# Two gated MLPs entered differently: the mixer's last products and the first plain pair in one loop, a second plain pair, no GpSimd work at the entries

## Chip, cores and metric

One core of a Trainium2 chip runs the whole program in one launch. The metric is the device time in microseconds (us); three runs of the kernel before took 2312.16, 2318.49 and 2319.06 us, so the median is 2318.49 us. TensorE (PE in the rows) multiplies matrices, VectorE (DVE), ScalarE (ACT) and GpSimd (POOL) work elementwise, and SyncE (SP) issues the DMAs.

## What is computed

The reference is an encoder of two layers on one sequence of 1024 frames with 1024 channels. Each layer is a mixer and a gated MLP, each behind an RMS norm and each added to the residual stream. The change touches only the seams between mixer and MLP:

```python
def conv_ffn(h, w_up, conv_w, conv_b, w_down):
    s = h.shape[1]
    u = h @ w_up                                  # 1024 -> 2 x 2816
    up = jnp.pad(u, ((0, 0), (CONV_WIDTH - 1, 0), (0, 0)))
    conv = conv_b
    for j in range(CONV_WIDTH):
        conv = conv + conv_w[j] * up[:, j:j + s]
    a, g = jnp.split(conv, 2, axis=-1)
    return (jax.nn.silu(a) * g) @ w_down
...
x = x + even_mixer(...)   # layer 0; ends in "... @ w_out"
x = x + conv_ffn(rms_norm(x, ffn_norm[layer]), ...)
x = x + odd_mixer(...)    # layer 1; ends in "... @ w_out"
x = x + conv_ffn(rms_norm(x, ffn_norm[layer]), ...)
```

## The kernel before

Everything is transposed: a tile has 128 channels on the partitions and 1024 frames along it, so the residual stream `x` is eight tiles, `x[0]` to `x[7]`. `T0` and `T1` are a tile's left and right 512 frames, and a product over 512 frames fills one bank of PSUM. TensorE works in the rounded 32-bit format fp32r; for accuracy each operand is split into a high part (ScalarE, a cast) and a low part (VectorE, a subtraction), and each product is three matmuls, high by high, high by low and low by high (`mm3`, L137, L139 and L141).

**End of a mixer.** The last two of eight inner tiles of the mixer's output product are applied tile by tile of `x`, in the order 0, 4, 1, 5, 2, 6, 3, 7 (`ORDER`): for each tile two halves of 2 x 3 matmuls into PSUM, then VectorE adds the bank to `x` (L745 in layer 0, L761 in layer 1). That is 8 x 12 = 96 matmuls.

**Norm and blocks.** After each tile `NormBlocks.add` stores `x` to DRAM for the later residual (L288), writes the tile times its gain as two split blocks (`blk`: high part by ScalarE at L282, low part by VectorE at L283), squares it on ScalarE (L302) and adds the square to a running sum (L303, on GpSimd for all but the last tile). Then ScalarE scales `x` itself by the gain (L304), for use in sums of blocks. `stats` (L254) sums the squares over the partitions by 16 tiny matmuls, ScalarE and VectorE turn that into 1/rms, a diagonal tile is built (L261), and `spread` (L268, L269) broadcasts it to `rstd_bc`.

**Up-projection.** There are 22 pairs of an `a` tile and a gate tile (`FT` = 22). Pair 0 is plain: all eight blocks against two weight tiles, 2 x 48 = 96 matmuls, loaded and split by `raw_a` (L781, L782). VectorE then multiplies the banks by `rstd_bc` (L909). Pairs 1 to 21 save products with a Strassen-like scheme (`Pair`, L823): seven products of 12 matmuls, 84 for a pair. It needs sums of the weights (`s12`, `s34`, L794 to L799, loaded two pairs ahead through `wraw` and `raw_g`) and sums of the blocks of `x` (L914 to L917, on GpSimd for two of four k and on VectorE for the other two), split into `T1` to `T4` (L803). Each finished pair goes through the convolution (L886 on ScalarE, L887 and L889 on VectorE), SiLU, and the product with the gate on GpSimd (L981), and is stored to DRAM. The convolution's results rotate through three buffers, `c`.

**What sets the order.** TensorE's instructions stand in program order. Those of the other engines are ordered at build time by a list scheduler; on the chip each engine runs its own list strictly in order and waits by semaphores. So an instruction that waits holds up all that stands behind it on its engine. PSUM has eight banks, two each for `lin`, `z`, `t` and `d`. The blocks and the mixer's last operands share 16 buffers, so the blocks of the last two tiles reuse those of the operands.

Of the kernel before, what the change touches and what calls it, by code (L numbers as in the profile page):

```python
# [56 lines left out]
def trunk_kernel(  # L57
# [213 lines left out]
    class NormBlocks(Norm):  # L271
# [14 lines left out]
        def add(self, m, x):  # L286
# [10 lines left out]
            if self.n == 1:  # L297
                self.acc = self.acc_tile()
                S.activation(self.acc, x, AF.Square)
            else:  # L300
                sq = self.sq_tile()
                S.activation(sq, x, AF.Square)  # L302
                (V if self.n == KT else G).tensor_tensor(self.acc, self.acc, sq, op=ALU.add)  # L303
            S.activation(x, x, AF.Copy, scale=g)  # L304
# [433 lines left out]
    for m in ORDER:  # L738
        sl = slice(m * P, (m + 1) * P)
        for i, cs in enumerate(HALVES):  # L740
            ps = bank(("lin", "z")[i])
            for n, k in enumerate(last):
                mm3([ps], (ws[n][0][:, sl], ws[n][1][:, sl]), ([mix[k][0][:, cs]], [mix[k][1][:, cs]]),
                    n == 0, n == len(last) - 1)
            V.tensor_tensor(x[m][:, cs], x[m][:, cs], ps, op=ALU.add)  # L745
        norm.add(m, x[m])
# [3 lines left out]
    def accumulate(ws, acts, tags, after=None, order=range(KT), together=1):  # L750
        order = list(order)
        n = len(ws)
        for ms in [order[:together]] + [[m] for m in order[together:]]:
            pss = {m: [bank(next(tags)), bank(next(tags))] for m in ms}
            for i, cs in enumerate(HALVES):
                for m in ms:
                    sl = slice(m * P, (m + 1) * P)
                    for k in range(n):
                        mm3([pss[m][i]], (ws[k][0][:, sl], ws[k][1][:, sl]),
                            ([acts[k][0][:, cs]], [acts[k][1][:, cs]]), k == 0, k == n - 1)  # L760
                    V.tensor_tensor(x[m][:, cs], x[m][:, cs], pss[m][i], op=ALU.add)  # L761
            if after is not None:
                for m in ms:
                    after(m)

    def ffn(layer, nm, after, onward=None):
# [72 lines left out]

        def scaled(dst, cs):  # L840
# [52 lines left out]
        pss = []  # L893
        for i in (0, FT):
            _, hi, lo = raw_a(i)
            ps = [bank(next(tags)), bank(next(tags))]
            for n, k in enumerate(ORDER):
                rt = (nm.b11[k], nm.b12[k]) if k < 4 else (nm.b21[k - 4], nm.b22[k - 4])
                sl = slice(k * P, (k + 1) * P)
                mm3(ps, (hi[:, sl], lo[:, sl]), ([t[:, T0] for t in rt], [t[:, T1] for t in rt]),  # L900
                    n == 0, n == KT - 1)
                if i and n == 3:
                    nm.stats(next(tags))
            pss.append(ps)
        nm.spread(tags)
        us = [slot(F32, "u") for _ in range(2)]
        for u, ps in zip(us, pss):
            for cs, b in zip(HALVES, ps):
                V.tensor_tensor(u[:, cs], b, rstd_bc[:, cs], op=ALU.mult)  # L909
        load_a(1)  # L910
        for k in range(4):
            E = TENG(k)
            lo_, hi_ = x[k], x[k + 4]
            E.tensor_tensor(lo_[:, T0], lo_[:, T1], lo_[:, T0], op=ALU.subtract)  # L914
            E.tensor_tensor(lo_[:, T1], hi_[:, T1], lo_[:, T1], op=ALU.subtract)
            E.tensor_tensor(hi_[:, T1], hi_[:, T1], lo_[:, T0], op=ALU.subtract)
            E.tensor_tensor(hi_[:, T0], hi_[:, T0], hi_[:, T1], op=ALU.subtract)  # L917
        sum12(1)
# [454 lines left out]
```

## Time and profile before

| | |
|---|---|
| median of three runs | 2318.49 us (2312.16 to 2319.06) |
| the profiled execution's own time | 2324.55 us |
| its span, first to last instruction | 2322.8 us |
| busy shares: PE, DVE, ACT, POOL | 96%, 72%, 44%, 18% |
| mean granted TensorE clock | 0.977 of full |
| entry of layer 0 (mixer's last products to end of pair 1) | 446.48 to 536.51 us |
| entry of layer 1 (the same) | 1598.12 to 1686.48 us |

A busy share is an average over stages. What the change touches are two stretches of some 90 us each, called the entries here, and a change there is worth what TensorE waits there, whatever the averages say. In a row of the timeline the first number is the start in us from the span's start, the second the length, then engine, source line, operation, output and inputs, and in brackets how long the engine was idle before and what ended that. A row of stretches has, for each engine, busy us and instructions, then the granted clock (PEclk), the DMA engines' share and GB/s.

### The profile page before, as it was taken

The numbers are of one execution on the slowest core, as the hardware profiler recorded it, in microseconds if no ns is written. First come the engines' busy times: TensorE is split into PE (matmuls) and PEld (weight loads), VectorE is DVE, ScalarE is ACT, GpSimd is POOL, SyncE is SP. The second block draws the span as 40 slices with busy tenths as digits, with TensorE's granted clock in tenths as the row PEclk, the third lists the DMA queues.
The fourth block names the chain that finished last, engine by engine and source line by source line (L and its number), as shares of the span: only waits on it lengthen the run. The fifth ranks groups of instructions, "written<-read, shape, count | busy, mean of one in ns | idle before, by whom it ended". The sixth has DMA issues, their size and how long they took to land.

```text
span 2322.8 us, 27350 instructions
## 1 busy us (share of the span) xinstructions
PE 2236.1 (96%) x10624; PEld 1840.3 (79%) x10624; DVE 1664.0 (72%) x2221; ACT 1031.8 (44%) x1561; POOL 421.6 (18%) x250
## 2 busy tenths in 40 slices
PE   8999889979999999999999999999799999999999
PEld 7878777758888887888887878787588888878887
DVE  5576588698999998745446555557999999986543
ACT  6666666454444444311146352527544444442210
POOL 2331350131111111512020000003211111124210
PEclk9999889979999999999999999999899999999999
DMA  3000112222222225522001111112222222254211
GB/s 140 19 29 20 38 35 99 87 82 73 82 82 82 82 82 177 183 85 91 10 28 41 34 46 36 41 43 87 68 82 82 82 82 82 82 199 163 95 51 73
DMA packets 51425, 178.52 MB, mean 77 GB/s; under 512 B 5968, under 2 KB 6608, under 8 KB 51296
## 3 DMA queue, kind: packets, MB, share of 16 engines
q1 hardware_dynamic: 51296, 176.78, 22.7%
q8 instruction: 83, 1.36, 0.2%
q14 instruction: 46, 0.38, 0.1%
HBM read 140.06 MB, written 36.70 MB: 76 GB/s over the span
## 4 chain that ended last, share of the span: by engine, by line
PE 82%; DVE 9%; issue 3%; ACT 3%; DMA 1%; POOL 0%; SPq 0%; DVEq 0%; ACTq 0%; POOLq 0%
PE lin L823 15%; PE z L823 10%; PE lin L137 5%; PE t L823 5%; PE d L823 5%; PE lin L139 5%; PE lin L141 5%; PE z L141 2%; PE t L139 2%; PE z L139 2%; PE z L137 2%; PE t L137 2%; PE t L141 2%; PE d L139 2%; PE d L137 2%
## 5 line engine op out<-in xcount | busy, mean ns | idle before, releaser
L123 ACT CAST whi<-wraw 128x1024 fp32r<-128x1024 f32 (+4 forms) x108 | 107.6, 998 | 356.5 <-PE d L139 233.3
L981 POOL TENSOR_TENSOR c<-c 128x1024 f32<-128x1024 f32 x44 | 108.3, 2461 | 757.9 <-ACT c L980 757.9
L841 DVE TENSOR_TENSOR u<-u,rstd_bc 128x512 f32<-128x512 f32 x168 | 168.2, 1002 | 2.8
L124 DVE TENSOR_TENSOR wlo<-wraw,whi 128x1024 fp32r<-128x1024 f32 (+3 forms) x94 | 137.3, 1460 | 35.2 <-ACT whi L123 34.3
L886 ACT ACTIVATE c<-u,prm 128x1024 f32<-128x1024 f32 x88 | 109.4, 1246 | 84.4 <-DVE u L841 74.3
L1010 POOL TENSOR_TENSOR act<-a,act 128x1024 fp32r<-128x1024 f32 x40 | 105.8, 2653 | 217.2 <-ACT act L1009 217.2
L610 DVE TENSOR_TENSOR_SCAN pt<-pt,z 128x128 f32<-128x128 f32 (+3 forms) x96 | 93.1, 970 | 55.7 <-ACT z L603 53.1
L137 PE MATMUL lin<-h_hi,whi 128*128 128x512 f32 x304 | 122.4, 441 | 5.9 <-ACT whi L123 5.9
L823 PE MATMUL d<-T,a 128*128 128x512 f32 x504 | 121.1, 389 | 0.0
L889 DVE SCALAR_TENSOR_TENSOR c<-u,prm,c 128x1022 f32<-128x1022 f32 x88 | 115.6, 1315 | 0.1
L887 DVE SCALAR_TENSOR_TENSOR c<-u,prm,c 128x1023 f32<-128x1023 f32 x88 | 112.4, 1279 | 2.9 <-ACT c L886 2.7
L761 DVE TENSOR_TENSOR x<-x,t 128x512 f32<-128x512 f32 x97 | 66.4, 685 | 65.5 <-PE t L141 65.4
L139 PE MATMUL lin<-h_lo,whi 128*128 128x512 f32 x304 | 111.7, 405 | 1.3 <-DVE h_lo L240 1.3
L141 PE MATMUL lin<-h_hi,wlo 128*128 128x512 f32 x304 | 111.7, 406 | 0.0
L823 PE MATMUL lin<-blk,whi 128*128 128x512 f32 x336 | 107.8, 403 | 3.2 <-DVE u L909 3.2
L823 PEld LDWEIGHTS d<-T,a 128*128 128x128 f32 x504 | 94.6, 188 | 19.6
L802 ACT CAST s12h<-s 128x1024 fp32r<-128x1024 f32 x42 | 44.2, 1054 | 146.1 <-PE lin L823 142.5
L823 PE MATMUL z<-blk,s34h 128*128 128x512 f32 x336 | 105.6, 395 | 2.8 <-DVE u L872 2.8
L761 DVE TENSOR_TENSOR x<-x,d 128x512 f32<-128x512 f32 x97 | 66.4, 685 | 58.0 <-PE d L141 58.0
L823 PE MATMUL z<-blk,s12h 128*128 128x512 f32 x336 | 105.7, 396 | 0.0
L823 PE MATMUL lin<-T,s12h 128*128 128x512 f32 x336 | 104.5, 392 | 0.0
L823 PE MATMUL t<-blk,whi 128*128 128x512 f32 x336 | 103.6, 390 | 0.0
(406 smaller groups left out, 6497.5 us busy)
## 6 DMA issues: line engine op xcount, KB each, us to landing
wraw<-in_wup SPq DMA_DIRECT2D x46, 512.0 KB, 3.6
act<-c SPq DMA_DIRECT2D x44, 512.0 KB, 2.6
wraw<-in_wdn SPq DMA_DIRECT2D x44, 512.0 KB, 3.7
raw_g<-in_wup SPq DMA_DIRECT2D x42, 512.0 KB, 3.6
a<-act SPq DMA_DIRECT2D x40, 512.0 KB, 4.3
xs<-x SPq DMA_DIRECT2D x16, 512.0 KB, 2.6
x<-xs SPq DMA_DIRECT2D x16, 512.0 KB, 5.0
x<-in_xT SPq DMA_DIRECT2D x8, 512.0 KB, 6.6
```

The lines of the kernel that those rows point to most:

```text
L123: S.copy(hi[:, cs], raw[:, cs])
L124: (eng or V).tensor_tensor(lo[:, cs], raw[:, cs], hi[:, cs].bitcast(F32), op=ALU.subtract)
L137: PE.matmul(out[i], wh, ah[i], start=first, stop=False)
L139: PE.matmul(out[i], wh, al[i], start=False, stop=False)
L141: PE.matmul(out[i], wl, ah[i], start=False, stop=last)
L761: V.tensor_tensor(x[m][:, cs], x[m][:, cs], pss[m][i], op=ALU.add)
L823: PE.matmul(ps, w, m, start=first and k == 0 and n == 0, stop=k == 3 and n == 2, skip_group_check=True)
L841: V.tensor_tensor(dst, dst, rstd_bc[:, cs], op=ALU.mult)
L886: S.activation(c, u, AF.Identity, scale=pcol(b + 2), bias=pcol(b + 3))
L887: V.scalar_tensor_tensor(c[:, 1:], u[:, :T - 1], pcol(b + 1), c[:, 1:], op0=ALU.mult, op1=ALU.add)
L889: V.scalar_tensor_tensor(c[:, 2:], u[:, :T - 2], pcol(b), c[:, 2:], op0=ALU.mult, op1=ALU.add)
L981: G.tensor_tensor(ca, ca, cg, op=ALU.mult)
```

## The change

- `NormBlocks.add` gives all its running sums to VectorE, and scales only tiles 0 to 3 of `x` by the gain. For tiles 4 to 7 the gain is folded into the sums of blocks (`rsums`), which now all run on VectorE: one plain and three scalar-tensor-tensor instructions for each k. GpSimd has nothing left at the entries: 14 instructions leave it for each.
- The weights of pair 0 are no longer loaded through `wraw` late; they go straight into `s12` and `s34` and are split into `s12h`, `s12l`, `s34h`, `s34l` ahead of the loop.
- One loop over the tiles: the mixer's products for two tiles ahead, then for each further tile its mixer products (12 matmuls), and behind them the plain products of pair 0 that read the blocks two tiles back (12 matmuls). Two more plain tiles follow the loop.
- Pair 1 is plain too. Its `a` tile runs between `stats` and `spread`, its gate tile behind `spread`. It costs 96 matmuls where the scheme took 84. Strassen pairs start at pair 2.
- In layer 1 the mixer's operands take buffers of the block pool and its second weight one of the general weight buffers, since the attention's pool is now closed before the loop.

```diff
-                (V if self.n == KT else G).tensor_tensor(self.acc, self.acc, sq, op=ALU.add)
-            S.activation(x, x, AF.Copy, scale=g)
+                V.tensor_tensor(self.acc, self.acc, sq, op=ALU.add)
+            if m < KT // 2:
+                S.activation(x, x, AF.Copy, scale=g)
...
+        def rsums(k):
+            lo_, hi_, g = x[k], x[k + 4], pcol(nm.col + k + 4)
+            V.tensor_tensor(lo_[:, T0], lo_[:, T1], lo_[:, T0], op=ALU.subtract)
+            V.scalar_tensor_tensor(lo_[:, T1], hi_[:, T1], g, lo_[:, T1], op0=ALU.mult, op1=ALU.subtract)
+            V.scalar_tensor_tensor(hi_[:, T1], hi_[:, T1], g, lo_[:, T0], op0=ALU.mult, op1=ALU.subtract)
+            V.scalar_tensor_tensor(hi_[:, T0], hi_[:, T0], g, hi_[:, T1], op0=ALU.mult, op1=ALU.subtract)
...
+        first = []
+        for i, hl, raw, tag in ((0, (s12h, s12l), s12, "lin"), (FT, (s34h, s34l), s34, "z")):
+            nc.sync.dma_start(raw, wup[layer, i])
+            split(*hl, raw)
+            first.append((hl, [bank(tag), bank(tag)]))
...
+        def first_tile(n):
+            for w, ps in first:
+                plain_tile(w, ps, n)
...
+        add_tiles(ow, mixt, otags, ORDER[:2])
+        for n, m in enumerate(ORDER):
+            if n >= 2:
+                add_tiles(ow, mixt, otags, [m])
+            nm.add(m, x[m])
+            if n >= 2:
+                first_tile(n - 2)
+        for k in range(4):
+            rsums(k)
+            for n in ("T4", "T2", "T3"):
+                rblock(n, k)
+        first_tile(KT - 2)
+        first_tile(KT - 1)
+        nm.stats("t")
+        ps = plain(1, "td")
+        nm.spread(iter("dt"))
...
+        for b in [b for _, b in first] + [ps]:
+            evacuate(b)
+        ps = plain(FT + 1, ("lin", "z"))
         for k in range(4):
-            E = TENG(k)
...
+            rblock("T1", k)
+        load_a(2)
...
-            g = gated(hd, oraw, ss)
+            g = gated(hd, oraw, ss, hpool, "h", 16)
...
-            accumulate(out_weights(hd), mixt, itertools.cycle("td"), lambda m: nnorm.add(m, x[m]), ORDER, 2)
+            ow = [load_split(woo[2 * hd]), load_split(woo[2 * hd + 1])]
```

**How the lists move.** Nothing moves outside the two entries. On TensorE in layer 0 the kernel before goes from the mixer's products of the last tile straight to pair 0, whose first weight is `whi`:

```order
L137 MATMUL z<-mh,whi 128x512
L139 MATMUL z<-ml,whi 128x512
L141 MATMUL z<-mh,wlo 128x512
L137 MATMUL lin<-blk,whi 128x512
L137 MATMUL z<-blk,whi 128x512
L139 MATMUL lin<-blk,whi 128x512
```

Now each tile's mixer products (`d<-mh`) have a tile of pair 0 behind them, out of `s12h` and `s34h`:

```order
L137 MATMUL d<-mh,whi 128x512
L139 MATMUL d<-ml,whi 128x512
L141 MATMUL d<-mh,wlo 128x512
L137 MATMUL lin<-blk,s12h 128x512 x2
L139 MATMUL lin<-blk,s12h 128x512 x2
L141 MATMUL lin<-blk,s12l 128x512 x2
L137 MATMUL z<-blk,s34h 128x512 x2
L139 MATMUL z<-blk,s34h 128x512 x2
L141 MATMUL z<-blk,s34l 128x512 x2
```

So 12 matmuls that wait only for blocks of two tiles back lie between any two additions to `x`.

On VectorE the same place in layer 0, now; `x_3543` and `x_4115` are tiles 0 and 4, `x_3635` is tile 1, and `blk_4498` and `blk_4501` are the left and the right block of tile 0:

```order
L751 TENSOR_TENSOR x_3543<-x_3543,t_4464 128x512
L751 TENSOR_TENSOR x_4115<-x_4115,t_4466 128x512
L283 SCALAR_TENSOR_TENSOR blk_4498<-x_3543,prm_77,blk_4498 128x512
L797 TENSOR_TENSOR s12l_4450<-s12_4447,s12h_4449 128x1024
L751 TENSOR_TENSOR x_3543<-x_3543,d_4465 128x512
L797 TENSOR_TENSOR s34l_4452<-s34_4448,s34h_4451 128x1024
L751 TENSOR_TENSOR x_4115<-x_4115,d_4467 128x512
L788 TENSOR_TENSOR s12_4447<-raw_g_4446 128x512
L797 TENSOR_TENSOR a22_4453<-raw_g_4446,a22_4453 128x512
L751 TENSOR_TENSOR x_3635<-x_3635,t_4518 128x512
L283 SCALAR_TENSOR_TENSOR blk_4501<-x_3543,prm_77,blk_4501 128x512
```

The two splits of pair 0's weights and two steps for pair 2 came in ahead of the right block of tile 0, which the first plain tile reads.

On ScalarE in layer 1, now, at the same place; `s12h_12812` is the high part of pair 0's first weight, whose load must wait for the attention's buffers, and `blk_12861` the first block:

```order
L1270 CAST mh_12734<-r32_12436 128x512
L1270 CAST mh_12736<-r32_12686 128x512
L796 CAST s12h_12812<-s12_12810 128x1024
L282 ACTIVATE blk_12861<-x_7553,prm_77 128x512
L796 CAST s34h_12814<-s34_12811 128x1024
```

The cast that waits for the load stands ahead of the first block.

More of the change, by code (lines that the diff above doesn't have):

```diff
@@ new lines, in first_tile, with plain @@
+        def first_tile(n):
+            for w, ps in first:
+                plain_tile(w, ps, n)
+        def plain(i, tags):
+            w, ps = raw_a(i)[1:], [bank(t) for t in tags]
+            for n in range(KT):
+                plain_tile(w, ps, n)
+            return ps
+        otags = itertools.cycle("td")
+        add_tiles(ow, mixt, otags, ORDER[:2])
[5 more added lines that the diff above has]
+                first_tile(n - 2)
@@ L947, in ffn @@
                 ua, ug = us[0], us[1]
+            elif i == 1:
+                ua, ug = us[2], us[0]
+                for cs, b in zip(HALVES, ps):
+                    V.tensor_tensor(ug[:, cs], b, rstd_bc[:, cs], op=ALU.mult)
             else:
@@ L1040, in trunk_kernel @@
     norm.sq_tile = lambda: slot(F32, "nsq")
-    ffn(0, n0, lambda m: norm.add(x[m]), onward)
+    ffn(0, n0, lambda m: norm.add(x[m]), ws, [mix[k] for k in last], onward)
     ev = ExitStack()
```

98 lines of the change are left out of this document (33 added, 65 removed).

## The prediction

> **What bounds the kernel now.** The page's row of engines gives TensorE 96% of the span, so only stretches in which it waits can yield anything. I then cut both entries into stretches (columns: us, then busy us of PE, PEld, DVE, ACT and POOL, the granted clock, DMA share, GB/s).
>
> ```profile
> PE 2236.1 (96%) x10624; PEld 1840.3 (79%) x10624; DVE 1664.0 (72%) x2221; ACT 1031.8 (44%) x1561; POOL 421.6 (18%) x250
> ```
>
> ```profile
> 460.40:474.20 13.80, 9.94 (x30) 7.01 (x30) 13.80 (x11) 8.93 (x12) 13.80 (x8) 0.78 0.28 115
> 474.20:490.00 15.80, 7.43 (x22) 5.46 (x22) 15.77 (x15) 10.62 (x14) 10.13 (x5) 0.65 0.28 100
> 490.00:511.20 21.20, 19.17 (x94) 15.80 (x92) 19.62 (x29) 12.30 (x17) 0.00 (x0) 1.00 0.24 75
> ```
>
> From 460.4 to 474.2 VectorE is busy all 13.80 us and so is GpSimd, while TensorE gets 30 matmuls done and its clock drops to 0.78. VectorE is the bound there. The waits of TensorE, first in entry 0, then in entry 1, name what it waits for:
>
> ```profile
> PE lin L141 <- DVE wlo L782: 5.4, 1, 5.4
> PE lin L137 <- DVE x L745: 3.9, 2, 2.7
> ...
> PE lin L139 <- DVE blk L283: 5.9, 1, 5.9
> ```
>
> Why VectorE is late, its rows tell. The same split of a block takes 0.75 us at 450.50 with GpSimd idle, and 2.29 us at 460.26 with GpSimd at work; the addition to `x`, which has one input in PSUM, keeps its 0.67 us beside it.
>
> ```profile
> 450.50 0.75 DVE L283 SCALAR_TENSOR_TENSOR blk<-x,prm,blk 128x512 fp32r<-128x512 f32 x1
> ...
> 459.67 0.67 DVE L745 TENSOR_TENSOR x<-x,z 128x512 f32<-128x512 f32 x1
> 460.26 2.29 DVE L283 SCALAR_TENSOR_TENSOR blk<-x,prm,blk 128x512 fp32r<-128x512 f32 x1
> ```
>
> ```profile
> L283 DVE SCALAR_TENSOR_TENSOR blk<-x,prm,blk 128x512 fp32r<-128x512 f32 x16 | 25.3, 1593 | 1.5 <-ACT blk L282 1.5
> ```
>
> In entry 0 the 16 splits take 25.3 us where 16 x 0.74 = 11.8 would do: 13.5 us lost beside GpSimd. The Trainium skill ("SBUF — State Buffer", Who interferes with whom) says that a VectorE instruction with two SBUF inputs and a GpSimd one that reads SBUF lock each other out; these rows agree.
>
> **What the entries last, and their floor.** TensorE's rows at both ends of each entry:
>
> ```profile
> 446.48 0.39 PE L137 MATMUL z<-mh,whi 128*128 128x512 f32 x1
> ...
> 459.85 0.39 PE L141 MATMUL lin<-mh,wlo 128*128 128x512 f32 x1
> ...
> 501.72 1.84 PE L254 MATMUL lin<-ones,nacc 128*128 128x2 f32 x16
> 503.43 0.47 PE L137 MATMUL t<-blk,whi 128*128 128x512 f32 x1
> ...
> 511.19 1.12 PE L268 MATMUL z<-ndg,ones 128*128 128x512 f32 x2 [2.03 <-DVE ndg L261]
> ...
> 514.74 1.22 PE L823 MATMUL lin<-blk,whi 128*128 128x512 f32 x2 [1.08 <-DVE u L909]
> ...
> 519.74 0.63 PE L823 MATMUL z<-blk,s12h 128*128 128x512 f32 x2
> ...
> 536.51 0.62 PE L823 MATMUL lin<-blk,whi 128*128 128x512 f32 x2
> ```
>
> ```profile
> 1598.12 0.48 PE L137 MATMUL t<-mh,whi 128*128 128x512 f32 x1
> ...
> 1686.48 0.62 PE L823 MATMUL lin<-blk,whi 128*128 128x512 f32 x2
> ```
>
> Entry 0 lasts 536.51 - 446.48 = 90.0 us, entry 1 lasts 1686.48 - 1598.12 = 88.4 us. At full clock 59 matmuls start in 459.85 - 446.48 = 13.37 us, 0.2267 us each. Before, an entry holds 96 + 96 + 84 = 276 of them, 62.6 us of work, so some 27 and 26 us go to waits, slow clock and the norm. After, it holds 96 + 96 + 96 = 288, 65.3 us: the plain second pair costs 12 x 0.2267 = 2.7 us for each entry, and nothing hides that, since it is TensorE's own work.
>
> **VectorE's account.** I price its list for an entry by the steps from start to start:
>
> ```profile
> 489.66 0.74 DVE L283 SCALAR_TENSOR_TENSOR blk<-x,prm,blk 128x512 fp32r<-128x512 f32 x1
> 490.32 0.68 DVE L917 TENSOR_TENSOR x<-x 128x512 f32<-128x512 f32 x1
> 490.92 0.68 DVE L803 TENSOR_TENSOR T<-x,T 128x512 fp32r<-128x512 f32 x1
> 491.52 1.22 DVE L303 TENSOR_TENSOR nacc<-nacc,nsq 128x1024 f32<-128x1024 f32 x1
> 492.66 0.68 DVE L914 TENSOR_TENSOR x<-x 128x512 f32<-128x512 f32 x1
> ```
>
> A half tile takes 0.60 us, with a gain in it 0.66, a whole tile 1.14. What comes over from GpSimd is six sums and eight sums of blocks: 6 x 1.14 + 2 x 0.60 + 6 x 0.66 = 12.0 us, less than the 13.5 us that go. The two other plain sums of blocks per k become scalar-tensor-tensor at 0.06 us more each; ScalarE loses four scalings. Up to the first use of `rstd_bc` VectorE then has 16 additions (9.6), 16 block splits (10.6), 7 sums (8.0), 16 sums of blocks (10.3), 12 splits T2 to T4 (7.2), 6 half tiles of weight sums (3.6) and 8 whole tiles, weight splits and the diagonal among them (9.1), with the reciprocal 58.6 us, from about 1.4 us behind the entry's start: done at 60.0. In the same time TensorE has 240 matmuls and the statistics, 54.4 + 1.7 = 56.1 us. So VectorE's load stays; what the change buys is that TensorE has 48 more matmuls to do meanwhile, and that these need blocks two tiles old instead of the last ones. Both are then nearly full, and every bubble of VectorE counts almost one to one.
>
> **What TensorE still waits for.** I walk the lists with these steps.
> - First plain tile: TensorE wants the low part of tile 0's right block 36 + 3 matmuls in, at 8.8 us. VectorE has, from 2.75 us on, six half-tile steps besides two block splits and the two weight splits ahead of it: 6 x 0.60 + 2 x 0.66 + 2 x 1.14 = 7.2 us, so 10.0. Wait: 1.2 us.
> - Seventh plain tile: its blocks take over buffers of the mixer's operands and so wait for the last mixer matmul. One plain tile (2.7 us) covers; VectorE needs 5.35 us from there (an addition, a sum of blocks and a weight split stand between), TensorE wants it at 3.4. Wait: 1.9 us.
> - The turn from pair 1's first tile over `spread` to its gate tile: cast and split of pair 2's weight stand ahead of the evacuation (1.05 + 1.14), then the evacuation and a second one, with the gaps between engines 3.4 us. It was 514.74 - 511.19 = 3.55 besides a wait of 2.03 ahead of it.
> - Pair 2: the convolution of pair 1's gate reuses a `c` buffer. ScalarE has it ahead of the copy that releases TensorE's seventh product, and it waits for GpSimd's product of pair 0 and its store:
>
> ```profile
> 526.80 1.28 ACT L980 ACT_TABLE_LOAD   x1
> 528.09 1.07 ACT L980 ACTIVATE c<-c 128x1024 f32<-128x1024 f32 x1
> ```
>
> ```profile
> 529.24 2.65 POOL L981 TENSOR_TENSOR c<-c 128x1024 f32<-128x1024 f32 x1 [41.37 <-ACT c L980]
> ```
>
> ```profile
> L886 ACT ACTIVATE c<-u,prm 128x1024 f32<-128x1024 f32 x88 | 109.4, 1246 | 84.4 <-DVE u L841 74.3
> ...
> act<-c SPq DMA_DIRECT2D x44, 512.0 KB, 2.6
> ```
>
> From pair 1's last matmul on, ScalarE casts a weight (1.05), loads a table (1.28) and does SiLU (1.07); GpSimd multiplies (2.65) and the store lands (2.6); then come the convolution (1.25), a cast (1.05) and the copy (half a cast and more, 0.6): 11.5 us, wanted behind four products of 12, at 10.9. With gaps I take 0.8; the ends are nothing and, with a store of twice the time, 3.4.
>
> Pair 0's weights cost nothing in entry 0. Their loads follow this one in SyncE's queue (the second row has how long such a load takes to land):
>
> ```profile
> 437.33 0.33 SPq L778 DMA_DIRECT2D wraw<-in_wup  x1
> ```
>
> ```profile
> wraw<-in_wup SPq DMA_DIRECT2D x46, 512.0 KB, 3.6
> ```
>
> Four loads of 3.6 us, even one after the other, are there 14.4 us on, at 451.7, and the first plain tile begins at 446.5 + 8.2 = 454.7; the splits are in VectorE's account. If that cover were gone, each us of delay would show, as in layer 1.
>
> Entry 0: 65.3 + 1.7 + 1.2 + 1.9 + 3.4 + 0.8 = 74.3 us, against 90.0: 15.7 us gained. Entry 1 adds two things.
>
> ```profile
> 1597.30 1.05 ACT L781 CAST whi<-wraw 128x1024 fp32r<-128x1024 f32 x1 [4.21 <-PE z L139]
> ...
> 1601.47 0.72 ACT L282 ACTIVATE blk<-x,prm 128x512 fp32r<-128x512 f32 x1
> ...
> 1598.96 1.22 DVE L782 TENSOR_TENSOR wlo<-wraw,whi 128x1024 fp32r<-128x1024 f32 x1
> ```
>
> The mixer's second weight now takes the place of that weight in the lists, so its low part is there at 1600.1, and TensorE wants it five matmuls in, at 1599.25: 0.9 us. And pair 0's weight can be loaded only when the attention's last transposes are over, about 1598.1; landing 3.6 us later its cast ends at 1602.8, and the first block, behind it on ScalarE, comes 1.4 us later than the row at 1601.47. With three loads at once it may land later: 0 to 6 us, I take 1.4, by the median landing. Entry 1: 74.3 + 0.9 + 1.4 = 76.6 against 88.4, gain 11.8. Together 27.5 us.
>
> **The clock.** Rows of entry 0 behind a wait:
>
> ```profile
> 468.94 0.79 PE L137 MATMUL lin<-mh,whi 128*128 128x512 f32 x1 [2.70 <-DVE x L745]
> 469.53 0.63 PE L139 MATMUL lin<-ml,whi 128*128 128x512 f32 x1
> ...
> 473.80 0.63 PE L141 MATMUL z<-mh,wlo 128*128 128x512 f32 x1
> ```
>
> After idle times of 2.70 and 2.03 us matmuls start every 4.27 / 10 = 0.427 us for a while; behind the `spread` the 12 up to 519.74 took 5.0 instead of 2.7 us. One such stretch costs 2.3 us. My waits are of 0.8 to 3 us, so I count one in the two entries: 27.5 - 2.3 = 25.2. The Trainium skill ("TensorE: Matmul & The Clock Gate", What's actually happening) has the slow clock follow an idle window of about 3.4 us; by that no wait of mine brings one, and the gain would be 27.5. The rows show it after shorter ones, and I go by them.
>
> The profiled execution took 2324.55 us, so the sum against it is 2299.4. It lies 6.1 us above the median of 2318.49; from that, 25.2 us less is 2293.
>
> **Rivals.**
> A bubble of VectorE in the trace, for the second:
>
> ```profile
> 500.42 0.69 DVE L795 TENSOR_TENSOR s<-s,wraw 128x512 f32<-128x512 f32 x1 [1.55 <-DMA wraw<-in_wup]
> ```
>
> 1. The waits vanish, as the lists have slack that my walk misses. Only work, statistics and a turn of 3.0 us remain, 70.0 us for each entry: gain 20.0 + 18.4, time 2280. For it: VectorE runs back to back for long where GpSimd is idle. Against: its 58.6 us are more than TensorE's 56.1. Chance 0.12.
> 2. VectorE trails: three bubbles in each entry like that one, 6 x 1.55 = 9.3 us, and three slow stretches more, 6.9 us, leave 9.0 us of gain: 2309. For it: ScalarE's list now interleaves splits, sums and stores that wait on one another. Against: TensorE's waits would leave VectorE time to catch up. Chance 0.18.
>
> 3. The long splits were not GpSimd's doing and stay: 13.5 us in each entry, on a full VectorE, 25.2 - 27.0, about 2320. Against it stand the rows at 459.67 and 460.26, and 490 to 511.2, where all splits are short. Chance 0.04.
> 4. Slower: the loop never warms up. If each of its tiles waits some 2 us for blocks, the clock stays low, and the 168 matmuls of each loop take 0.2 us more each: 67 us. From 126 of these 336 on the gain is gone; all of them give 2318 - 25 + 67 = 2360. Against: each tile has 24 x 0.2267 = 5.4 us of TensorE's work, and what VectorE must do for it is 2 x 0.60 + 2 x 0.66 + 1.14 = 3.7 us, so waits come at single tiles. Chance 0.05.
>
> **The numbers.** The forecast, a single walk with its own errors of 8 us, has 0.61; its time is 2293. The range reaches to rivals 1 and 2, from 2280 to 2309, as bubbles and slow stretches may come in any number between. A measurement of this kernel tells about 0.3% or 7 us from no change. Faster by more: 0.61 + 0.12 + 0.18, less 0.01 for the end of rival 2 near no change, 0.90; the same 0.05; slower 0.05.
>
> **What would show it.** GpSimd without a row in both entries; all block splits near 0.74 us; entries of about 74 and 77 us; VectorE still busy nearly throughout; TensorE's waits at the first and the seventh plain tile and at pair 1's gate tile, no longer a 5 us one. Splits that stay long would refute the first step; an entry of over 85 us with short splits, the account of VectorE; a difference outside the entries, the whole frame.

## The result, and the profile after

The kernel after takes 2294.32 us (median of four runs, 2291.6 to 2299.12), the kernel before 2318.76 us in the runs beside it: a ratio of 0.99, with an interval of 0.9885 to 0.9915, so 24.4 us less, where the prediction had 25.2. Run again later (e11), the kernel after took 2294.37 us, a ratio of 0.9903 (0.9883 to 0.9923).

The row of engines on the page of the kernel after shows GpSimd's share gone down and TensorE's up by one point:

```profile
PE 2221.9 (97%) x10648; PEld 1830.4 (80%) x10648; DVE 1642.7 (72%) x2229; ACT 1018.0 (44%) x1543; POOL 364.6 (16%) x222
```

The stretches of the kernel after, entry 0, pair 2 behind it, entry 1, pair 2 behind it (us, then busy us of PE, PEld, DVE, ACT and POOL, the granted clock, DMA share, GB/s):

```profile
439.60:513.10 73.50, 70.58 (x309) 56.40 (x308) 71.48 (x99) 45.98 (x60) 0.00 (x0) 1.00 0.25 87
513.10:535.30 22.20, 19.85 (x86) 15.64 (x86) 18.52 (x18) 9.88 (x12) 5.61 (x2) 1.00 0.20 71
1573.20:1648.30 75.10, 71.12 (x311) 56.42 (x309) 74.31 (x104) 47.96 (x64) 0.00 (x0) 1.00 0.30 105
1648.30:1671.90 23.60, 21.19 (x86) 16.82 (x85) 18.60 (x18) 9.92 (x12) 5.71 (x2) 0.93 0.22 69
```

The same four of the kernel before:

```profile
445.10:536.50 91.40, 75.89 (x297) 58.60 (x296) 82.26 (x92) 53.86 (x70) 31.57 (x15) 0.87 0.23 81
536.50:555.80 19.30, 19.30 (x86) 15.81 (x85) 18.10 (x20) 9.09 (x11) 2.41 (x1) 1.00 0.26 84
1598.10:1686.50 88.40, 73.02 (x300) 56.43 (x299) 82.83 (x96) 54.29 (x73) 32.21 (x15) 0.92 0.26 90
1686.50:1705.70 19.20, 19.20 (x85) 15.76 (x84) 18.10 (x20) 8.98 (x11) 2.41 (x1) 1.00 0.29 86
```

Entry 0 begins 1.4 us earlier here than in the prediction: the first six matmuls of tile 0 write a bank that bears the same name, `lin`, as the stage ahead of them, and were counted there as part of that stage. So entry 0 lasted 91.4 us before, not 90.0. The entries lose 17.9 and 13.3 us; pair 2, untouched by the change itself, gains 2.9 and 4.4. Together 218.3 - 194.4 = 23.9 us, which is what the medians say. VectorE is busy 97% of entry 0 where it was 90%, and the granted clock is 1.00 where it was 0.87 and 0.92. The two profiled executions differ by more, 33.0 us; the other 9 us lie in parts that the change doesn't touch, and runs of one kernel differ by as much (those of the kernel before, beside e1 to e4, lie between 2310.26 and 2325.61).

The waits of TensorE in the kernel after, entry 0 and then entry 1 (total, times, longest):

```profile
PE lin L139 <- DVE blk L283: 2.0, 2, 1.2
PE lin L137 <- DVE u L940: 0.8, 1, 0.8
```

```profile
PE lin L139 <- DVE blk L283: 2.3, 2, 1.6
PE lin L137 <- DVE u L940: 0.8, 1, 0.8
PE t L141 <- DVE wlo L124: 0.7, 1, 0.7
```

The block splits of entry 0 are short now (count; ns of one: least, median, longest), where the kernel before had 737, 1514 and 2945 ns:

```profile
L283 DVE SCALAR_TENSOR_TENSOR blk<-x,prm,blk x16: 747/754/764, 443.1 to 481.9; 128x512 fp32r<-128x512 f32 x16
```

The waits of 5.4 and 5.9 us are gone, and what is left are the waits that the walk named: the first and the seventh plain tile (L139), the gate tile of pair 1 (L137) and, in layer 1, the low part of the mixer's second weight.

### The profile page after: what moved, and what is told of

Same layout as the page of the kernel before. It is cut to its first block, busy times and chain, and to the rows that moved or that the text cites. A ratio compares the mean times of both kernels' runs of the same rounds, so it can differ in the third digit from the quotient of the medians.

```text
span 2289.9 us, 27345 instructions
## 1 busy us (share of the span) xinstructions
PE 2221.9 (97%) x10648; PEld 1830.4 (80%) x10648; DVE 1642.7 (72%) x2229; ACT 1018.0 (44%) x1543; POOL 364.6 (16%) x222
## 4 chain that ended last, share of the span: by engine, by line
PE 68%; DVE 3%; issue 3%; ACT 2%; DMA 1%; POOL 0%; ACTq 0%; POOLq 0%; DVEq 0%
PE lin L817 14%; PE z L817 9%; PE d L817 5%; PE t L817 4%; PE lin L137 3%; PE lin L139 3%; PE lin L141 3%; PE z L137 3%; PE z L141 3%; PE z L139 3%; PE t L137 2%; PE d L137 2%; PE d L139 2%; PE t L139 2%; PE t L141 2%
## 5 line engine op out<-in xcount | busy, mean ns | idle before, releaser
L843 DVE TENSOR_TENSOR u<-u,rstd_bc 128x512 f32<-128x512 f32 x160 | 160.4, 1004 | 2.6
L888 ACT ACTIVATE c<-u,prm 128x1024 f32<-128x1024 f32 x88 | 109.6, 1245 | 76.8 <-DVE u L843 71.3
L137 PE MATMUL lin<-h_hi,whi 128*128 128x512 f32 x304 | 121.4, 437 | 6.3 <-ACT whi L123 6.2
L891 DVE SCALAR_TENSOR_TENSOR c<-u,prm,c 128x1022 f32<-128x1022 f32 x88 | 120.3, 1367 | 0.1
L751 DVE TENSOR_TENSOR x<-x,t 128x512 f32<-128x512 f32 x105 | 72.0, 686 | 66.9 <-PE t L141 66.8
L817 PE MATMUL d<-T,a 128*128 128x512 f32 x480 | 115.5, 389 | 0.0
L751 DVE TENSOR_TENSOR x<-x,d 128x512 f32<-128x512 f32 x105 | 72.0, 686 | 57.5 <-PE d L141 57.5
L139 PE MATMUL lin<-h_lo,whi 128*128 128x512 f32 x304 | 110.9, 403 | 1.2 <-DVE h_lo L240 1.2
L817 PE MATMUL z<-blk,s34h 128*128 128x512 f32 x320 | 100.7, 396 | 4.6 <-DVE u L874 4.6
L817 PE MATMUL lin<-T,s34h 128*128 128x512 f32 x320 | 99.9, 394 | 3.5 <-ACT tm L865 3.5
L817 PE MATMUL z<-blk,s12h 128*128 128x512 f32 x320 | 100.7, 396 | 0.0
L817 PE MATMUL lin<-blk,whi 128*128 128x512 f32 x320 | 99.8, 393 | 0.0
L817 PE MATMUL lin<-T,s12h 128*128 128x512 f32 x320 | 99.5, 392 | 0.0
```

Source lines behind the costliest of these rows:

```text
L137: PE.matmul(out[i], wh, ah[i], start=first, stop=False)
L139: PE.matmul(out[i], wh, al[i], start=False, stop=False)
L817: PE.matmul(ps, w, m, start=first and k == 0 and n == 0, stop=k == 3 and n == 2, skip_group_check=True)
L843: V.tensor_tensor(dst, dst, rstd_bc[:, cs], op=ALU.mult)
L888: S.activation(c, u, AF.Identity, scale=pcol(b + 2), bias=pcol(b + 3))
L891: V.scalar_tensor_tensor(c[:, 2:], u[:, :T - 2], pcol(b), c[:, 2:], op0=ALU.mult, op1=ALU.add)
```

## The experiments

All kernels, by rows of their traces: us of each entry, to the end of pair 1, and of pair 2 behind it; the sum of the four; the median; the ratio to the kernel before, run beside it.

| kernel | entry 0 | pair 2 | entry 1 | pair 2 | sum | median | ratio (interval) |
|---|---|---|---|---|---|---|---|
| before | 91.4 | 19.3 | 88.4 | 19.2 | 218.3 | 2318.76 | |
| after | 73.5 | 22.2 | 75.1 | 23.6 | 194.4 | 2294.32 | 0.99 (0.9885 to 0.9915) |
| after, again (e11) | 73.7 | 22.0 | 75.1 | 23.1 | 193.9 | 2294.37 | 0.9903 (0.9883 to 0.9923) |
| before without GpSimd (e1) | 84.1 | 19.3 | 85.7 | 19.3 | 208.4 | 2307.13 | 0.9967 (0.9956 to 0.9978) |
| after with GpSimd (e2) | 84.5 | 22.1 | 86.3 | 23.5 | 216.4 | 2318.18 | 1.0003 (0.9992 to 1.0013) |
| one plain pair (e3) | 84.2 | 19.3 | 87.6 | 19.3 | 210.4 | 2314.11 | 0.9978 (0.9963 to 0.9993) |
| not interleaved (e9) | 79.1 | 22.1 | 82.9 | 24.1 | 208.2 | 2300.71 | 0.9943 (0.9922 to 0.9965) |
| more VectorE (e5) | 82.8 | 22.2 | 84.0 | 19.2 | 208.2 | 2309.82 | 0.9967 (0.9951 to 0.9982) |
| less VectorE (e6) | 72.6 | 22.2 | 74.1 | 23.5 | 192.4 | 2292.89 | 0.9895 (0.9873 to 0.9917) |
| `c` exchanged (e4) | 73.6 | 19.2 | 75.1 | 19.3 | 187.2 | 2285.75 | 0.9873 (0.986 to 0.9886) |
| e4, lag of three (e7) | 72.9 | 24.0 | 74.5 | 19.2 | 190.6 | 2291.43 | 0.9883 (0.9865 to 0.99) |
| e7, early spread (e8) | 70.5 | 19.6 | 72.9 | 21.0 | 184.0 | 2297.85 | 0.9916 (0.9896 to 0.9937) |
| e4, early spread (e10) | 72.2 | 21.0 | 74.8 | 19.5 | 187.5 | 2290.41 | 0.9885 (0.9861 to 0.9909) |
| e4, weights later (e12) | 75.2 | 19.2 | 76.6 | 19.3 | 190.3 | 2288.14 | 0.9881 (0.9857 to 0.9906) |

**Each part alone.** First the order before, with GpSimd's work given to VectorE (e1):

```diff
-                (V if self.n == KT else G).tensor_tensor(self.acc, self.acc, sq, op=ALU.add)
+                V.tensor_tensor(self.acc, self.acc, sq, op=ALU.add)
...
-        return G if k < 2 else V
+        return V
```

> The kernel before, with its GpSimd work at the entries (running sums, half of the block sums) given to VectorE, and the order of TensorE's work as it was. Theory: the splits shorten to 0.75 us (13.5 us less in entry 0), but VectorE takes over about 12 us, so its load stays, and TensorE has nothing more to do meanwhile: entries of 85 to 90 us, time 2310 to 2320 us. Rival (the long splits alone were the loss, the loop over tiles is decoration): entries near 76 us and a time of 2292 to 2298 us.

Then the kernel after with GpSimd's work put back (e2):

```diff
-                V.tensor_tensor(self.acc, self.acc, sq, op=ALU.add)
-            if m < KT // 2:
-                S.activation(x, x, AF.Copy, scale=g)
+                (V if self.n == KT else G).tensor_tensor(self.acc, self.acc, sq, op=ALU.add)
+            S.activation(x, x, AF.Copy, scale=g)
...
+            E, lo_, hi_ = G if k < 2 else V, x[k], x[k + 4]
+            E.tensor_tensor(lo_[:, T0], lo_[:, T1], lo_[:, T0], op=ALU.subtract)
...
```

> The kernel after, with the running sums, all scalings of tiles and half of the block sums as before, GpSimd included, and the new loop kept. Theory: splits stretch again to some 1.5 to 2.3 us wherever GpSimd runs beside them, and with VectorE full each entry grows by 5 to 13 us: 2304 to 2320 us. Rival (the loop alone brings the gain, since TensorE has other work while VectorE is late): entries within 2 us of 73.6 and 75.1, time 2292 to 2298 us.

The 16 block splits of entry 0 (ns of one: least, median, longest), in e1 and then in e2:

```profile
L283 DVE SCALAR_TENSOR_TENSOR blk<-x,prm,blk x16: 741/742/746, 446.3 to 480.1; 128x512 fp32r<-128x512 f32 x16
```

```profile
L283 DVE SCALAR_TENSOR_TENSOR blk<-x,prm,blk x16: 737/960/2891, 448.9 to 497.0; 128x512 fp32r<-128x512 f32 x16
```

Without GpSimd all are 0.74 us, in the old order too; with it single ones go to 2.9 us again, in the new one too. So the stretching is GpSimd's doing. But taking GpSimd away is worth 9.8 us by itself (2316.93 us for the kernel before beside it; 9.9 by rows), of 24.4. The largest waits left in entry 0 of e1 show why:

```profile
PE lin L141 <- DVE wlo L782: 4.3, 1, 4.3
PE z L268 <- DVE ndg L261: 2.0, 1, 2.0
PE z L137 <- DVE x L745: 1.4, 2, 1.2
PE lin L137 <- ACT whi L781: 1.3, 1, 1.3
```

The split of pair 0's weight is still late, by 4.3 us instead of 5.4. And e2, the loop and both plain pairs with GpSimd, gains nothing that can be told: its entries are 11 us longer than those of the kernel after. It gives ScalarE its four scalings of `x` back too; how much of the 11 us is theirs, no run tells. My theory held for e2; for e1 it gave too little (it said 2310 to 2320), the rival far too much. Neither part makes the gain alone.

**The second plain pair** (e3) taken away, pair 1 by the scheme again:

```diff
-        ps = plain(1, "td")
...
-        ps = plain(FT + 1, ("lin", "z"))
+        us.append(slot(F32, "u"))
...
-        load_a(2)
+        load_a(1)
```

> The kernel after, but only pair 0 is plain; pair 1 goes by the scheme with 12 matmuls fewer, and the spread follows the statistics at once. Theory: VectorE needs about 60 us to the end of its list, TensorE has only 192 matmuls (43.5 us) and waits for the rest; with turn and a pair of 19.3 us each entry takes about 83 us instead of 73.6 and 75.1, and the 2.9 and 4.3 us that pair 2 loses go: 5 to 13 us slower than after, 2299 to 2307 us. Rival (the plain pair only costs its 12 matmuls of 0.2267 us, VectorE has slack): 5.4 us for the matmuls and some 7 us of pair 2's waits less, 2280 to 2290 us.

Measured 2314.11 us: 12 matmuls fewer in each layer, and 19.8 us slower than the kernel after, 16.0 by rows. The rows of TensorE at the spread in e3:

```profile
490.71 1.95 PE L254 MATMUL t<-ones,nacc 128*128 128x2 f32 x16 [0.91 <-DVE nacc L303]
503.33 2.07 PE L268 MATMUL d<-ndg,ones 128*128 128x512 f32 x2 [10.67 <-DVE ndg L261]
```

TensorE stands idle for 10.67 us until the diagonal tile, 60.9 us after the entry's start at 442.40; the account had 60.0. In the kernel after, the 48 matmuls of pair 1's first tile fill this time. The second plain pair puts 2.7 us of work in the place of 10.7 us of waiting. My theory was right in kind and too small in size: it had 2299 to 2307 us and 83 us for each entry, and got 84.2 and 87.6, since in layer 1 that wait came to 12.85 us.

**The interleaving** (e9) taken away, all mixer products ahead of pair 0's:

```diff
             nm.add(m, x[m])
-            if n >= 2:
-                first_tile(n - 2)
+        for n in range(KT - 2):
+            first_tile(n)
```

> The kernel after, but the mixer's products of all eight tiles run ahead of the plain products of pair 0, as in the kernel before; weights, second plain pair and VectorE's work as in the kernel after. Theory of the record (the interleaved 12 matmuls are what TensorE does while VectorE catches up): TensorE waits for VectorE's additions in the mixer's tiles, which come every 2.7 us where VectorE needs 3.7 for one, up to 8 x 1.0 us and some slow clock: 4 to 8 us more for each entry, 2302 to 2310 us. Rival (the waits come early, but the diagonal tile was ready 6 us ahead of its use, and with no wait at the first and the seventh plain tile the entry is as long as before): entries within 1.5 us of 73.6 and 75.1, 2291 to 2297 us.

Measured 2300.71 us, between the two and just under the theory's range of 2302 to 2310; by rows the entries grow by 5.6 and 7.8 us, as the theory had it, but not where it had it. The waits of entry 0 in e9, and the stretch from the statistics to the spread, first of e9 and then of the kernel after:

```profile
PE t L254 <- DVE nacc L303: 3.0, 1, 3.0
PE lin L137 <- DVE u L940: 0.8, 1, 0.8
PE t L137 <- DVE x L751: 0.6, 1, 0.6
PE d L137 <- DVE x L751: 0.3, 1, 0.3
```

```profile
487.40:503.50 16.10, 16.10 (x65) 13.65 (x66) 10.82 (x16) 5.39 (x8) 0.00 (x0) 0.79 0.09 30
```

```profile
486.40:499.10 12.70, 12.70 (x66) 10.82 (x65) 12.70 (x19) 6.52 (x10) 0.00 (x0) 1.00 0.29 83
```

In the mixer's tiles e9 waits for 0.9 us only. It then runs through pair 0 without a wait and meets VectorE's last sum in one piece of 3.0 us (4.8 in layer 1); the clock drops to 0.79 and the same work takes 3.4 us more (4.5 in layer 1). The statistics start 48.9 us after the entry's start (438.46) against 46.8: up to there the interleaving saves 2.1 us (3.4 in layer 1), and it cuts the rest into pieces that leave the clock at full.

**Is VectorE full?** Eight us more of it (e5), and 6.8 us less (e6):

```diff
                 V.tensor_tensor(self.acc, self.acc, sq, op=ALU.add)
+                V.tensor_tensor(sq, sq, sq, op=ALU.add)
```

> The kernel after, with one more VectorE instruction on a whole tile ahead of each running sum, 7 x 1.14 = 8.0 us of VectorE for each entry, on a buffer whose sum is not touched otherwise (it doubles the square: the norm leaves out the right scale, nothing else changes in the work). Theory of the record (VectorE nearly full, each us counts): the seventh plain tile and the statistics come 5 to 8 us later in each entry, 2304 to 2310 us. Rival (the trace of after shows the diagonal tile ready 6 us ahead of the spread; that slack is there throughout): 0 to 2 us for each entry, 2294 to 2298 us.

In the kernel that ran the extra instruction stands behind the running sum, as in the diff, on a square that nothing reads any more; contrary to the words of the expectation, the norm is left whole.

```diff
-                V.tensor_tensor(self.acc, self.acc, sq, op=ALU.add)
+                if self.n == KT:
+                    V.tensor_tensor(self.acc, self.acc, sq, op=ALU.add)
```

> The kernel after, which leaves out six of the seven running sums of squares (so the norm sees only two tiles), 6 x 1.14 = 6.8 us of VectorE less for each entry, TensorE's work as it was. Theory (TensorE's entry is near its own floor, and of VectorE's lateness only the waits of 0.8 to 1.6 us at the first and the seventh plain tile are left): 1 to 2 us less for each entry, 2290 to 2293 us. Rival (VectorE alone sets the entry's length): 5 to 7 us less for each, 2280 to 2284 us.

Entry 0 of e5 and of e6:

```profile
439.80:522.60 82.80, 74.94 (x309) 59.07 (x308) 79.37 (x106) 46.80 (x60) 0.00 (x0) 0.96 0.21 77
```

```profile
437.30:509.90 72.60, 70.46 (x310) 56.56 (x309) 64.90 (x93) 45.77 (x60) 0.00 (x0) 1.00 0.24 88
```

8.0 us more cost 9.3 and 8.9 us; 6.8 us less gain 0.9 and 1.0. The theory held both times, though e5 cost more than the 5 to 8 us it had: in entry 0 TensorE's waits grow by 5.0 us, from 2.8 to 7.8, and most of the rest is the clock, which is granted at 0.96. In the kernel after the two engines are nearly balanced: what was added to VectorE's list cost its whole length, and of what was taken away only the wait at the seventh plain tile came back as time. The waits at the first plain tile (1.2 us) and the gate tile (0.8 us) hang on steps that e6 leaves in place.

**Pair 2.** The one thing that became worse. ScalarE in pair 2 of layer 0, then in layer 1, in the kernel after:

```profile
520.79 1.06 ACT L1008 ACTIVATE c<-c 128x1024 f32<-128x1024 f32 x1 [3.99 <-DVE c L891]
522.64 1.24 ACT L888 ACTIVATE c<-u,prm 128x1024 f32<-128x1024 f32 x1 [0.80 <-DMA act<-c]
523.79 1.03 ACT L796 CAST s12h<-s 128x1024 fp32r<-128x1024 f32 x1
524.73 0.58 ACT L865 COPY tm<-lin 128x512 f32<-128x512 f32 x1
```

```profile
1659.20 1.24 ACT L888 ACTIVATE c<-u,prm 128x1024 f32<-128x1024 f32 x1 [2.04 <-DMA act<-c]
```

The convolution (L888) reuses a buffer that the store of pair 0's product (`act<-c`) still reads, and the copy that TensorE's seventh product waits for (L865) stands two instructions behind it. The product itself comes late as well. GpSimd's row and a VectorE row beside it:

```profile
516.40 3.22 POOL L1009 TENSOR_TENSOR c<-c 128x1024 f32<-128x1024 f32 x1 [163.88 <-ACT c L1008]
```

```profile
517.26 3.43 DVE L891 SCALAR_TENSOR_TENSOR c<-u,prm,c 128x1022 f32<-128x1022 f32 x1
```

Both are longer than elsewhere (2.65 and 1.28 us). So two causes were to be told apart, the store and the product. e4 exchanges the two buffers of pair 0, so that the one which is reused is free once the product has read it:

```diff
             if i == 0:
+                ca, cg = cg, ca
```

> The kernel after, with the two convolution buffers of pair 0 exchanged, so that the one which pair 1's gate convolution takes over is free when GpSimd's product has read it, and no longer when the store of the product has landed. Theory (the wait for the store delays ScalarE's copy, and with it TensorE's seventh product in pair 2): pair 2 goes from 22.2 and 23.6 us to about 20.5 and 19.5, 4 to 6 us less in all, 2288 to 2291 us. Rival (the copy is late for GpSimd's product itself, locked with VectorE's convolution): pair 2 within 0.7 us of what it is, 2293 to 2296 us.

ScalarE's convolution in e4, and pair 2 in both layers:

```profile
523.75 1.25 ACT L888 ACTIVATE c<-u,prm 128x1024 f32<-128x1024 f32 x1 [2.93 <-POOL c L1011]
```

```profile
517.20:536.40 19.20, 19.20 (x85) 15.76 (x84) 18.30 (x18) 9.94 (x12) 6.56 (x2) 1.00 0.26 85
...
1651.50:1670.80 19.30, 19.30 (x86) 15.83 (x85) 18.39 (x18) 9.98 (x12) 6.61 (x2) 1.00 0.25 85
```

The convolution now starts 6.6 us into pair 2 (517.17) instead of 9.5 (513.14), though the product is as long as it was. TensorE waits no more, and pair 2 takes what every pair takes: 7.2 us less by rows, 2285.75 us, more than the theory had promised (2288 to 2291). So the dependence on the store was the cause, but its own wait, 0.80 and 2.04 us, is only a part of the gain. The exchange also changed the order of ScalarE's list. In the kernel after, the SiLU at 520.79 stands ahead of the convolution and waits 3.99 us for the VectorE row of 3.43 us above; in e4 it stands behind it:

```profile
524.90 1.05 ACT L1010 ACTIVATE c<-c 128x1024 f32<-128x1024 f32 x1
```

No run has the one without the other, so how much each is worth stays open.

None of e4's four runs (2283.95 to 2289.52) reaches the ten of the kernel after (2290.01 to 2299.12), six of which come from the kernel after run once more (e11), on the chip of e9 and e10. No run of both on one chip is on record; against the kernel before, run beside each, e4 takes 31.2 us less, the kernel after 24.4 and 21.0:

> The kernel after once more, unchanged, on the same chip as the two others: 2291 to 2299 us, and the same waits at the same rows. If it comes out near 2286 us, the exchange of the buffers was a difference between chips.

It gave the times and the waits of the first run, but for that of 2.41 us in pair 2 of layer 1, which came to 1.89.

**What is left of the waits.** Three tries to take the small waits away on top of e4. The lag of three tiles (e7), and the spread 12 matmuls earlier with it (e8) and without (e10):

```diff
-            if n >= 2:
-                first_tile(n - 2)
+            if n >= 3:
+                first_tile(n - 3)
...
+        first_tile(KT - 3)
```

> The kernel after with the exchanged convolution buffers, and the plain products of pair 0 three tiles behind the mixer's instead of two; so 12 matmuls more, 2.7 us, stand ahead of the first and of the last two plain tiles. Theory (the waits of 1.2 and 1.6 us at the first and of 0.8 us at the seventh plain tile are a lateness of VectorE that 2.7 us cover): 2 us less in the first entry and 2.3 in the second, 2281 to 2283 us beside 2285.75 for the exchange alone. Rival (VectorE must first add the third tile to the residual, and what it owes is only asked for one place later): waits of the same size at other rows, 2284 to 2288 us.

```diff
-        def plain(i, tags):
+        def plain(i, tags, spread=None):
             w, ps = raw_a(i)[1:], [bank(t) for t in tags]
             for n in range(KT):
+                if n == spread:
+                    nm.spread(iter("dt"))
                 plain_tile(w, ps, n)
...
-        ps = plain(1, "td")
-        nm.spread(iter("dt"))
+        ps = plain(1, "td", KT - 2)
```

> As the run before with the lag of three, and the broadcast of the norm put 12 matmuls before the end of pair 1's first tile, since the diagonal tile was ready 6 us before it was used. Theory: the gate tile's wait of 0.8 us for the first evacuation goes in both entries, 1.6 us less than the run before, 2279 to 2282 us. Rival (the diagonal tile comes later with the lag of three, or the evacuation is held up by the copies of the broadcast): no less than the run before, or up to 2 us more.

> The kernel after with the exchanged convolution buffers, a lag of two tiles as it was, and the broadcast of the norm 12 matmuls before the end of pair 1's first tile. Theory: the diagonal tile is ready by then, and the gate tile's wait of 0.8 us for the first evacuation goes in both entries; nothing else moves: 1.6 us less than the exchange alone, 2283 to 2285 us beside 2285.75. Rival (the copies and evacuations of the broadcast come between other work of VectorE and ScalarE, and pair 2 or the pairs behind it pay for it): 2286 to 2298 us.

In all three the entries became shorter than e4's, by 0.3 to 3.1 us, and the time did not. The waits from entry 0 to pair 2 in e7, and those in the 20 pairs behind entry 1 in e8:

```profile
PE lin L817 <- ACT tm L858: 2.3, 1, 2.3
PE lin L137 <- DVE u L941: 1.8, 1, 1.8
PE z L817 <- DVE blk L797: 0.5, 1, 0.5
PE lin L139 <- DVE blk L283: 0.3, 2, 0.2
```

```profile
PE z L817 <- DVE u L874: 8.2, 8, 1.6
```

In entry 0 of e7 the first tile's wait is gone, but the gate tile waits 1.8 us instead of 0.8 and pair 2 of layer 0 takes 24.0 us. In e8 the entries are the shortest of all, and eight waits in the pairs behind them, where e4 has a single one of 1.4 us, give 8.2 us back: VectorE's list there is in another order, though the edit is far away, and the sum that must come before the next weight is loaded (L793) stands 9.3 us into pair 5 instead of 7.9 (1724.44 - 1715.19 and, in e4, 1717.27 - 1709.34). In e10 pair 2 takes 1.8 and 0.2 us more and entry 1 is only 0.3 us shorter. The rivals were nearer each time, but e7 (2291.43 us) and e8 (6.4 us above e7) came out above their ranges too, 2284 to 2288 us and at most 2 us more; how far e7 and e10 differ from e4 in time the intervals don't tell.

The last run (e12), on top of e4, tests one step of the walk by itself. A copy of two columns delays the load of pair 2's gate weight, and with it two steps of VectorE that stand ahead of tile 0's right block:

```diff
             raws[i], *A[i] = raw_a(i)
+            if i == 2:
+                V.tensor_copy(raw_g[:, 0:2], x[6][:, 512:514])
             nc.sync.dma_start(raw_g, wup[layer, FT + i])
```

> The kernel after with the exchanged convolution buffers, and the gate weight of pair 2 loaded later: a VectorE copy of two columns out of a late sum of blocks into its buffer stands ahead of the load, so that its first sum and the split of its half (1.2 us of VectorE) no longer stand ahead of tile 0's right block. Theory (the first plain tile waits for VectorE's list, step by step, as in the walk of the record): its wait of 1.2 us in the first entry goes, and that of 1.6 us in the second falls to 0.4 or less; entries near 72.4 and 73.9 us, 2282 to 2285 us beside 2285.75 for the exchange alone. Rival (the block is late for another reason, its addition to the residual or ScalarE's cast): the wait stays within 0.3 us. What can go wrong: the weights of pair 2 come too late for it, and pair 2 takes over 19.3 us.

The waits of e12, first in entry 0, then in entry 1:

```profile
PE lin L137 <- DVE u L942: 2.0, 1, 2.0
PE lin L139 <- DVE blk L283: 0.8, 1, 0.8
```

```profile
PE lin L137 <- DVE u L942: 1.9, 1, 1.9
PE lin L139 <- DVE blk L283: 1.2, 2, 0.8
PE t L141 <- DVE wlo L124: 0.7, 1, 0.7
```

The first plain tile's wait of 1.2 us is gone in entry 0, and that of 1.6 us is down to 0.38 in entry 1 (1.2 less the seventh tile's 0.8), just as the theory said. But the steps are owed all the same: they come ahead of the first evacuation now, and the gate tile waits 2.0 and 1.9 us instead of 0.8. Behind that the clock falls:

```profile
499.30:503.20 3.90, 1.92 (x6) 0.61 (x4) 3.90 (x6) 1.96 (x3) 0.00 (x0) 1.00 0.00 0
503.20:516.20 13.00, 12.90 (x49) 10.24 (x50) 12.12 (x16) 6.21 (x8) 0.00 (x0) 0.87 0.14 42
```

The gate tile's 48 matmuls take 13.0 us where the kernel after needs 11.4 (501.76 to 513.14). So the mechanism of the theory is shown and its time is not: the entries became 1.6 and 1.5 us longer than e4's, and it took 2288.14 us instead of 2282 to 2285.

The best version is e4. By rows it takes 7.2 us off the kernel after and 31.1 off the kernel before.

## Why the prediction was right, step by step

- **GpSimd stretches VectorE's splits:** shown, by e1 and e2 from both sides.
- **The gain comes from TensorE having other work meanwhile:** shown, by what is lost without each part. Without the second plain pair most of it is lost (e3), without the interleaving some of it (e9), and with GpSimd all of it (e2). The prediction called the second pair a cost of 2.7 us that nothing hides, and its 48 matmuls ahead of the spread what the change buys; e3 shows both, 2.7 us of work for 10.7 us of waiting.
- **VectorE's account:** right in sum, wrong in order. From 441.12 to its first evacuation at 501.02 VectorE has 58.8 us of work, where the account had 58.6. It had the diagonal tile done 60.0 us into the entry. It is done at 493.0, 53.4 us in, since the scheduler puts ten steps for pair 2 behind it; it stands ready 6.1 us before the spread. "Every bubble of VectorE counts almost one to one" holds for what was added (e5), not for what was taken away (e6).
- **The first plain tile:** 1.2 us forecast, 1.22 measured, and e12 shows that the steps named ahead of it are the cause. In layer 1 the late weight load was to add 1.4; the wait is 1.56, so it added 0.3. The low part of the mixer's second weight: 0.9 forecast, 0.72 measured.
- **The seventh plain tile:** 1.9 forecast, 0.78 measured. **The turn over the spread:** 3.4 forecast, 501.76 - 499.06 = 2.70 measured. These two are 1.8 us too high; against them stand 1.7 us that are in no term: of the 73.5 us, matmuls, statistics, waits and turn make 65.3 + 1.8 + 2.0 + 2.7 = 71.8. Part of the rest are the slower starts behind each wait (after that of 1.22 us the next matmul starts 0.33 us on, 449.82 to 450.15). So entry 0 came to 73.5, as forecast without pair 2's share.
- **Pair 2, the mis-sized term:** "with gaps I take 0.8; the ends are nothing and, with a store of twice the time, 3.4." It cost 2.9 and 4.4 us. The chain was the right one (e4 removes it), but two links were priced by undisturbed rows: the product took 3.2 us, not 2.65, beside VectorE's convolution, and the store landed 2.9 us after its issue in layer 0 and 4.2 in layer 1, not 2.6. A load is issued 0.43 us behind the store in both layers (520.07 and 1655.37), so why the one in layer 1 took longer stays open. The chain also left out that the SiLU ahead of the convolution waits for VectorE (3.99 us at 520.79). A wait of 1.3 us for L874 in layer 0 came on top, behind a weight split of VectorE that took 3.10 us (528.05) beside GpSimd's next product (527.67), where the one at 516.13 took 1.22; and so did a slow stretch in layer 1.
- **The clock:** one slow stretch of 2.3 us was counted for the two entries; there is one, of 1.8 us, but in pair 2 of layer 1: the 36 matmuls behind the wait of 2.41 us took 10.0 us instead of 8.2. That one came at all was chance: e2 waits 2.37 us at the same place and keeps its clock (last section).

The errors cancel. By rows the entries and pair 2 gained 15.0 and 8.9 us, where the sum had 15.7 and 11.8 less 2.3. From its 25.2 us one comes to the 23.9 of the rows so: 1.4 more, as entry 0 of the kernel before was longer than it had it; 0.7 more, as entry 1 took 75.1 us instead of 75.8 without pair 2; 5.7 less, as pair 2 cost 7.3 us in all instead of 1.6; and 2.3 more, as the slow stretch lies in pair 2 and is counted there. So the mechanism was right and the entries were sized well, but that 25.2 lies within a microsecond of the measured 24.4 is in part luck.

## What to carry to other kernels

When two engines are both nearly full, an edit is worth what it lets the other engine do meanwhile: 12 more matmuls in each of two layers saved 16 us by rows, and GpSimd's removal alone, with all splits at 0.74 us, was worth less than half of the change. Follow a step that is moved to the place where it is owed next; e7, e10 and e12 each took a wait away and met it, or a longer one, a few us later (e10 in pair 2). And a buffer that a store reads is free only when the store has landed: let the next writer take over one that only an engine reads.

## What the runs showed of the hardware

The clock falls after shorter waits than the Trainium skill ("TensorE: Matmul & The Clock Gate", What's actually happening) leads one to think: it names an idle window of about 3.4 us. The length agrees with what the traces show; that such a window has to be idle throughout does not. In all fourteen traces the granted clock is either full or half, and within a trace it changes only at points that lie whole multiples of 3.4133 us apart: in e12 it falls at 504.94 and 1638.16 and rises at 508.35 and 1641.58, and 1638.16 - 504.94 = 1133.22 = 332 x 3.4133. So what counts is not how long a wait is, but how much idle time lies between two such points. In pair 2 of layer 1 the kernel after waits 2.41 us, of which 2.2 lie in one such stretch, and the next stretch is at half clock:

```profile
1659.69:1663.10 3.41, 1.19 (x5) 1.02 (x6) 2.63 (x3) 3.12 (x4) 0.00 (x0) 1.00 0.07 26
1663.10:1666.52 3.42, 3.42 (x10) 2.64 (x9) 3.42 (x3) 0.03 (x1) 2.29 (x1) 0.50 0.00 0
```

At the same place e2 waits 2.37 us, but the point at 1687.72 cuts this wait into 0.7 and 1.7 us, and the clock stays full:

```profile
1684.31:1687.72 3.41, 2.73 (x13) 1.91 (x11) 0.00 (x0) 1.47 (x2) 0.00 (x0) 1.00 0.67 201
1687.72:1691.13 3.41, 1.73 (x7) 1.42 (x8) 3.16 (x3) 2.58 (x4) 0.00 (x0) 1.00 0.00 0
1691.13:1694.54 3.41, 3.41 (x16) 2.82 (x15) 3.41 (x3) 0.59 (x1) 2.40 (x1) 1.00 0.01 2
```

In the entries and the pairs of all traces, a stretch at full clock with up to 1.70 us of idle time (e5, 482.43 to 485.84) is followed by another one at full clock, and one with 1.73 us (e12, 501.53 to 504.94) or more by one at half clock. There are three exceptions: one of 1.93 us in the kernel before (1656.03 to 1659.44) left the clock full, and two of 0.91 and 0.94 us in e3, which also hold the tiny matmuls of the statistics, halved it. A stretch at half clock cost 1.6 to 1.9 us (e12's gate tile 13.0 us instead of 11.4; pair 2 of layer 1 in the kernel after, 10.0 instead of 8.2, and in e11, 10.1). So a wait of some 1.7 us or more costs its own length or, by where it falls, 1.6 to 1.9 us more, and shorter pieces don't bring this on: the 3.0 us in one piece in e9 brought the half clock, the 1.22 and 0.78 us of the kernel after did not.
